# One transformer layer on one core: transposes set one by one between filler products, the causal mask between two score products, another order of the first loads with zero products ahead, and another order of the second and third norm

## The chip, the core and the metric

The kernel runs on one core of one Trainium2 chip. The time is the device time of one execution in microseconds (us), and the one compared is the median of several executions. The engines are named as the profile names them: PE multiplies matrices (PEld loads its weights), DVE and ACT work element by element, POOL and SP issue transfers here, and each of the five follows its own list of instructions in order, waiting on semaphores of the others.

## What is computed

The input is 1024 tokens of 1024 channels. The reference, cut to what matters:

```python
h = rmsnorm(x, g_pre_mix)
proj = h @ w_in                                   # u_pool (512) and q, k, v (8 heads of 64)
y_pool = multiscale_pool(u_pool, ...) @ w_br_pool
# stick-breaking attention, strictly causal, per head:
z = (q @ k.T) / 8
log_1mb = where(mask, log_sigmoid(-z), 0)
tail = cumsum(log_1mb, reverse=True) - log_1mb
o = where(mask, exp(log_sigmoid(z) + tail), 0) @ v
y_sb = o @ w_br_sb
gates = sigmoid(h @ w_gate + b_gate)
x = x + rmsnorm((gates[:1024] * y_pool + gates[1024:] * y_sb) @ w_out, g_post_mix)
h2 = rmsnorm(x, g_pre_mlp)
x = x + rmsnorm(square(relu(h2 @ w_up)) @ w_down, g_post_mlp)
```

## The kernel before, in words

**Number format.** Every large matrix and every activation is split into a part `hi` (a cast, ACT) and a rest `lo` (a subtraction, DVE). One product of the model is then three products on PE, `hi` by `hi`, `lo` by `hi` and `hi` by `lo`, all added into one PSUM bank (`mm3`, lines 105 to 114). A dense product of one weight tile with 512 tokens takes eight such steps (`dense_steps`), 24 matmuls. Channels lie on the partitions, tokens on the free axis, in two halves of 512 tokens (`h` is 0 or 1).

**Stages.** Everything is one straight program, but the order in which the instructions stand on each engine is made by a scheduler that simulates the program when it is built; the order of the code is a priority to it, and `issue_after(i)` forbids it to put an instruction ahead of `i`.

1. *First projection* (`phase_in`, from line 250). SP loads `vt` (gains), then in turn pieces of the first weight tile `u0` and tiles of `x` (eight of 128 by 512 for each half), then the tiles `u1` and `u2` whole. POOL loads the constants `eye`, `eyeb`, `maskb`, `rcnt` and `wm`. For each of the eight `k`, ACT makes `hT_hi` (L280), DVE `hT_lo` (L281), ACT a square (L287), which DVE adds up. PE runs the products of `u0`, `u1`, `u2` (tiles `du`, `zu`) with the first half, then with the second, and in between the sum of squares (`ms`) and the transpose of the row factors (`rt`).
2. *Pooling mixer* beside the last projections of this stage and the first `q`, `k`.
3. *Attention* (`phase_attention`). Heads 0 to 7, for each four pairs of query blocks, the longest first. `att_scores` makes the scores of one block: for each piece of at most 512 keys a product with `q`, one with `qs` (the halves of `q` exchanged), and for the last piece a third one that adds the mask (`eyeb` by `maskb`, L510). ACT makes two sigmoids (`T`, `F`), DVE a scan over `F` (L517) and a product (L518). `F` is one buffer, the score banks `z` are two. `att_out` then, per pair of key blocks `m`, transposes four (on the diagonal three) 128 by 128 squares of the two `T` tiles into the bank `at` (L534), lets `pump` run some filler work, splits `at` into `ahi` (ACT, L541) and `alo` (DVE, L542), and multiplies by `v` (four matmuls into `o`, L547).
   The *filler* is the dense products of the gates and of later heads' `q`, `k`, `v`. A credit of steps is given out: `w_out` steps (2.3) at each `m`, and the rest of the head's steps over the score blocks (`w_in`). Each filler step may not run ahead of the fourth last mark, a mark being set by the scores, the transposes and `o`.
4. *Branches and output projection* (`phase_post`): eight tiles `out` with each half. After a half is done, its `chain` runs beside the following products: norm 2 (`ms`, L762), residual, sum of squares, norm 3 (`ms`, L780), and the split into the operands of the MLP (`b_hi`, `b_lo`, lines 746 to 748). `beside` and `tick` tie the parts of the chain to steps of PE: the numbers behind `yield` are steps.
5. *MLP* (`phase_mlp`, `down`): the products of a seven-product scheme. The first 32 half products read `b11` (channels 0 to 511) and `b21` (512 to 1023) of the first half of the tokens, for each of 16 `up` tiles both; then come the sums and products of the other operands, then `w_down`, then the last norm.

Of the kernel before, what the change touches and what calls it, by code (L numbers as in the profile page):

```python
# [28 lines left out]
LAG = 4  # L29
P = 128  # L30
# [19 lines left out]
class Block:  # L50
    def __init__(self, tc, x, w, wmix, vec, eye, eyeb, maskb, rcnt, out):
# [9 lines left out]
        self.marks = []  # L61


    def prep(self, key, g, pieces=(), load=None, stash=None):
# [9 lines left out]
        for a, b in zip(edges, edges[1:]):  # L74
# [5 lines left out]
            for i in range(a, b, n):  # L80
                c = slice(i, i + n)
                nc.scalar.copy(hi[:, c], raw[:, c])  # L82
                nc.vector.tensor_sub(lo[:, c], raw[:, c], hi[:, c].bitcast(F32))  # L83
# [19 lines left out]

    def mm3(self, ps, terms, first=True, last=True):
        nc = self.nc
        n = len(terms)
        for i, (wh, wl, rh, rl) in enumerate(terms):
            if self.pin and len(self.marks) >= LAG:
                with self.tc.issue_after(self.marks[-LAG].ins):
                    nc.tensor.matmul(ps, wh, rh, start=first and i == 0, stop=False)  # L110
            else:
                nc.tensor.matmul(ps, wh, rh, start=first and i == 0, stop=False)  # L112
            nc.tensor.matmul(ps, wh, rl, start=False, stop=False)  # L113
            nc.tensor.matmul(ps, wl, rh, start=False, stop=last and i == n - 1)  # L114
# [54 lines left out]
    def build(self):  # L169
# [46 lines left out]

        nc.scalar.preload_act_table_set(TABLES)
# [6 lines left out]
        self.vt = cp.tile([P, N_VEC], F32, name="vt")  # L224
        nc.sync.dma_start(self.vt, self.vec)
        self.gn = cp.tile([P, 32], F32, name="gn")
        nc.vector.tensor_scalar(out=self.gn, in0=self.vt[:, 0:32], scalar1=-0.5, scalar2=None, op0=ALU.mult)
# [22 lines left out]
    def phase_in(self):  # L250
# [7 lines left out]
        todo = [(0, 0, 1), (0, 1, 1), (0, 2, 2)]  # L258
        self.prep(*self.order[0], pieces=(256, 512), load=lambda: load(*todo.pop(0)))
        self.next_prep = 1  # L260
        self.weights(("u", 1), 0)
        load(0, 4, 2)
        load(0, 6, 2)
        self.weights(("u", 2), 0)
        for k in range(0, NK, 2):
            load(1, k, 2)
        for t, src in zip((self.eye, self.eyeb, self.maskb, self.rcnt), self.consts):
            nc.gpsimd.dma_start(t, src)
# [75 lines left out]
        nc.gpsimd.dma_start(wm, self.wmix)  # L344
# [144 lines left out]
    def att_scores(self, h, i):  # L489
# [13 lines left out]
        for c, n in pieces:  # L503
# [4 lines left out]
            nc.tensor.matmul(z[:, c : c + n], qs[:, tt], k[:, c : c + n], start=False, stop=not last)  # L508
            if last:
                nc.tensor.matmul(z[:, w - P : w], self.eyeb, self.maskb, start=False, stop=True)  # L510
# [10 lines left out]
    def att_out(self, h, g, a):  # L521
# [4 lines left out]
        for m in range(g + 1):  # L526
# [4 lines left out]
            for b, (s, tt) in enumerate(((2 * m + 1, 0), (2 * m + 1, 1), (2 * m, 0), (2 * m, 1))):  # L531
                if diag and b == 0:
                    continue
# [723 lines left out]
```

## Time and profile before

| | us |
|---|---|
| median of three runs (lowest, highest) | 1316.82 (1315.09, 1317.61) |
| the profiled execution, its own time | 1318.3 |
| its span, first to last instruction | 1316.5 |
| PE busy | 1283.5 |
| DVE busy | 913.7 |
| ACT busy | 603.1 |

The profiled execution took 1.8 us more than its span, and 1.5 us more than the median. In the rows of a timeline the first number is the start in us from the span's beginning, the second the time until the last one of the row ended, then engine, line, operation, output and inputs, shape and count; the bracket tells how long the engine had stood idle, and who ended that. A matmul's time holds its way through the array; the pace of PE is read from one start to the next. In a table by windows the columns are the stretch, its length, the busy time of PE, PEld, DVE, ACT and POOL with their counts, the granted share of the PE clock, and the share and rate of the DMA engines. In the list of waits stand the waiting instruction, the one waited for, the total, the number of times and the longest.

### The profile page before, as it was taken

Reading aid. Unit: us, or ns where it says so; the run is one execution under the profiler, and the core shown is the slowest. Engines: PE = TensorE matmul, PEld = TensorE weight load, DVE = VectorE, ACT = ScalarE, POOL = GpSimd, SP = SyncE. Lnnn points to the kernel's source line nnn. Section 1 sums busy time; section 2 is a strip of 40 time slices with the busy share of each in tenths; the row PEclk is TensorE's granted clock in tenths of the full one; section 3 lists DMA queues with packets and bytes.
Section 4 is the critical chain, followed back from the end, with each engine's and each line's share of the span. In section 5 each row is a group of like instructions: output and inputs, shape, how many; then the busy total and the mean of one; then the engine's idle time right before and its main releaser. Section 6 shows DMA issues by size and latency. Waiting matters only on the chain.

```text
span 1316.5 us, 16672 instructions
## 1 busy us (share of the span) xinstructions
PE 1283.5 (97%) x6200; PEld 1069.4 (81%) x6200; DVE 913.7 (69%) x1234; ACT 603.1 (46%) x921; POOL 141.2 (11%) x281
## 2 busy tenths in 40 slices
PE   7999999998999999999999999999999999999995
PEld 5888888887888888888878887888888888888885
DVE  7686586676676664663577959877775654776975
ACT  7144455454555543223345736554465433344341
POOL 0001202100211222100001002211121000001000
PEclk9999999999999999999999999999999999999998
DMA  6243635623746969543146667766559555557741
GB/s 220 65 160 109 209 98 160 129 64 72 153 130 196 258 212 243 176 161 111 51 173 224 193 238 247 249 204 204 192 192 356 188 185 200 195 178 243 238 159 64
DMA packets 75089, 233.79 MB, mean 178 GB/s; under 512 B 8448, under 2 KB 10768, under 8 KB 72832
## 3 DMA queue, kind: packets, MB, share of 16 engines
q1 hardware_dynamic: 47216, 143.70, 33.2%
q0 software_dynamic: 27216, 88.50, 22.3%
q8 instruction: 49, 0.80, 0.2%
q10 hardware_dynamic: 576, 0.52, 0.1%
q14 instruction: 32, 0.26, 0.1%
HBM read 178.16 MB, written 83.89 MB: 199 GB/s over the span
## 4 chain that ended last, share of the span: by engine, by line
PE 82%; DVE 9%; issue 3%; ACT 2%; DMA 2%; SPq 0%; POOL 0%; DVEq 0%; ACTq 0%; POOLq 0%
PE d L112 18%; PE d L113 18%; PE d L114 18%; PE dg L110 4%; PE dg L114 4%; PE dg L113 4%; PE o L547 3%; PE at L534 2%; DVE F L517 2%; PE dqk L114 1%; PE dqk L113 1%; DVE T L518 1%; PE dqk L110 1%; PE z L505 1%; PE z L508 1%
## 5 line engine op out<-in xcount | busy, mean ns | idle before, releaser
L113 PE MATMUL d<-blo,whi 128*128 128x512 f32 (+1 forms) x456 | 172.7, 379 | 0.0
L114 PE MATMUL d<-bhi,wlo 128*128 128x512 f32 (+1 forms) x456 | 171.9, 378 | 0.0
L112 PE MATMUL d<-bhi,whi 128*128 128x512 f32 (+1 forms) x456 | 168.6, 378 | 0.0
L517 DVE TENSOR_TENSOR_SCAN F<-F,one 128x896 f32<-128x896 f32 (+3 forms) x64 | 86.8, 1357 | 46.5 <-ACT F L515 46.0
L82 ACT CAST whi<-wraw 128x512 fp32r<-128x512 f32 (+2 forms) x93 | 71.1, 791 | 82.1 <-PE d L113 30.8
L110 PE MATMUL dg<-hT_hi,whi 128*128 128x512 f32 x256 | 106.0, 414 | 0.0
L114 PE MATMUL dg<-hT_hi,wlo 128*128 128x512 f32 x256 | 101.2, 395 | 0.0
L113 PE MATMUL dg<-hT_lo,whi 128*128 128x512 f32 x256 | 100.6, 393 | 0.0
L83 DVE TENSOR_TENSOR wlo<-wraw,whi 128x512 fp32r<-128x512 f32 (+2 forms) x93 | 81.4, 897 | 27.3 <-ACT whi L82 27.2
L114 PEld LDWEIGHTS d<-bhi,wlo 128*128 128x128 f32 x456 | 85.8, 188 | 16.2 <-issue 0.2
L113 PEld LDWEIGHTS d<-blo,whi 128*128 128x128 f32 x456 | 85.7, 188 | 16.1 <-issue 0.2
L112 PEld LDWEIGHTS d<-bhi,whi 128*128 128x128 f32 x456 | 85.5, 188 | 16.0
L542 DVE TENSOR_TENSOR alo<-at,ahi 128x512 fp32r<-128x512 f32 (+1 forms) x80 | 50.5, 632 | 47.2 <-ACT ahi L541 46.5
L112 PE MATMUL d<-b_hi,whi 128*128 128x512 f32 x196 | 76.5, 394 | 3.6 <-ACT b_hi L747 2.7
L113 PE MATMUL d<-b_lo,whi 128*128 128x512 f32 x196 | 77.3, 396 | 0.0
L114 PE MATMUL d<-b_hi,wlo 128*128 128x512 f32 x196 | 75.6, 394 | 0.0
L1024 DVE TENSOR_TENSOR wlo<-slots_hi,whi 128x1024 fp32r<-128x1024 f32 x29 | 35.5, 1224 | 53.3 <-ACT whi L1022 53.3
L1022 ACT CAST whi<-slots_hi 128x1024 fp32r<-128x1024 f32 x29 | 30.5, 1052 | 83.2 <-PE d L113 63.7
L541 ACT CAST ahi<-at 128x512 fp32r<-128x512 f32 (+1 forms) x80 | 43.6, 544 | 48.8 <-PE at L534 47.8
L1022 ACT CAST whi<-slots_lo 128x1024 fp32r<-128x1024 f32 x27 | 28.4, 1053 | 72.9 <-PE d L113 59.2
L1024 DVE TENSOR_TENSOR wlo<-slots_lo,whi 128x1024 fp32r<-128x1024 f32 x27 | 33.0, 1222 | 36.8 <-ACT whi L1022 36.8
L514 ACT ACTIVATE T<-z 128x896 f32<-128x896 f32 (+3 forms) x64 | 42.3, 661 | 32.2 <-PE at L534 20.3
(302 smaller groups left out, 3305.0 us busy)
## 6 DMA issues: line engine op xcount, KB each, us to landing
wraw<-w SPq DMA_DIRECT2D x82, 512.0 KB, 4.3
wscr<-w POOLq DMA_DIRECT2D x24, 1024.0 KB, 9.8
ext_b<-ascr SPq DMA_DIRECT2D x40, 512.0 KB, 4.5
gscr<-gs POOLq DMA_DIRECT2D x32, 256.0 KB, 4.7
gate<-gscr POOLq DMA_DIRECT2D x16, 512.0 KB, 3.6
pscr<-p SPq DMA_DIRECT2D x32, 256.0 KB, 3.6
braw<-w SPq DMA_DIRECT2D x16, 512.0 KB, 5.6
ascr<-c POOLq DMA_DIRECT2D x32, 256.0 KB, 4.8
```

Of the source, the lines that this page charges most:

```text
L82: nc.scalar.copy(hi[:, c], raw[:, c])
L83: nc.vector.tensor_sub(lo[:, c], raw[:, c], hi[:, c].bitcast(F32))
L110: nc.tensor.matmul(ps, wh, rh, start=first and i == 0, stop=False)
L112: nc.tensor.matmul(ps, wh, rh, start=first and i == 0, stop=False)
L113: nc.tensor.matmul(ps, wh, rl, start=False, stop=False)
L114: nc.tensor.matmul(ps, wl, rh, start=False, stop=last and i == n - 1)
L514: nc.scalar.activation(tl[:, :w], z[:, :w], AF.Sigmoid)
L517: nc.vector.tensor_tensor_scan(fr, fr, self.one1.to_broadcast([P, w]), 1.0, ALU.mult, ALU.mult)
L541: nc.scalar.copy(hi[:, c0:], at[:, c0:])
L542: nc.vector.tensor_sub(lo[:, c0:], at[:, c0:], hi[:, c0:].bitcast(F32))
L1022: last_split[0] = nc.scalar.copy(hi, src).ins
L1024: last_split[1] = nc.vector.tensor_sub(lo, src, hi.bitcast(F32)).ins
```

## The change

It has five parts.

1. *First loads.* `u0`, `u1` and `u2` are loaded in three pieces each, in turn with `x`, their first pieces by POOL; the first tile of `x` leads SP's queue, ahead of `vt`; the constants and `wm` go behind `x` on SP. The splits of the weights follow piece by piece.
2. *Zeros first.* DVE clears a tile, and PE multiplies it by itself nine times (128 by 512, bf16, into a bank that nobody reads) at the very beginning.
3. *Attention, transposes.* Only the first transpose of a group stands by itself; each of the others is put right behind one of the next filler matmuls (`between`), and the filler matmul after it may not pass it. What is left over after `pump` is issued then. `w_out` goes from 2.3 to 3.3.
4. *Attention, mask.* The mask product stands between the products with `q` and `qs` of the last piece, not behind both.
5. *Norms 2 and 3 and the start of the MLP.* For the first half, the scaling of channel block `e` in norm 3 may not run ahead of the split of block `e - 2` (`done[-2]`), so that splits and scalings alternate; the sum of norm 3 is put three steps earlier (`yield 28`); for the second half, the scaling and residual of norm 2 may not run ahead of the last weight split so far (`last_lo`). The first four half products of the MLP are both `b11` ones of the tiles 0 and 1, then both `b21` ones.

```diff
@@ mm3
         for i, (wh, wl, rh, rl) in enumerate(terms):
-            if self.pin and len(self.marks) >= LAG:
-                with self.tc.issue_after(self.marks[-LAG].ins):
-                    nc.tensor.matmul(ps, wh, rh, start=first and i == 0, stop=False)
...
+            after = self.marks[-LAG].ins if self.pin and len(self.marks) >= LAG else None
+            for j, (a, b) in enumerate(((wh, rh), (wh, rl), (wl, rh))):
+                with self.behind(after):
+                    m = nc.tensor.matmul(ps, a, b, start=first and i + j == 0, stop=last and i == n - 1 and j == 2)
+                after = None
+                if self.between:
+                    with self.behind(m.ins):
+                        after = self.between.pop(0)().ins
@@ phase_in
-        todo = [(0, 0, 1), (0, 1, 1), (0, 2, 2)]
-        self.prep(*self.order[0], pieces=(256, 512), load=lambda: load(*todo.pop(0)))
...
+        for g in range(3):
+            load_w(nc.gpsimd, g, 0, 256)
+        load(0, 0, 1)
+        nc.sync.dma_start(self.vt, self.vec)
...
+        load(0, 1, 1)
+        load_w(nc.sync, 0, 256, 512)
+        load(0, 2, 1)
+        load_w(nc.sync, 1, 256, 512)
+        load_w(nc.sync, 2, 256, 512)
+        load(0, 3, 1)
+        load_w(nc.sync, 0, 512, 1024)
         load(0, 4, 2)
+        load_w(nc.sync, 1, 512, 1024)
+        load_w(nc.sync, 2, 512, 1024)
         load(0, 6, 2)
...
         for t, src in zip((self.eye, self.eyeb, self.maskb, self.rcnt), self.consts):
-            nc.gpsimd.dma_start(t, src)
+            nc.sync.dma_start(t, src)
+        zero = pa.tile([P, H], BF16, name="zero")
+        nc.vector.memset(zero, 0.0)
+        idle = self.zps.tile([P, H], F32, name="idle", tag="o", bufs=1)
+        for _ in range(9):
+            nc.tensor.matmul(idle, zero[:, :P], zero, start=True, stop=True)
@@ att_scores
-            nc.tensor.matmul(z[:, c : c + n], qs[:, tt], k[:, c : c + n], start=False, stop=not last)
             if last:
-                nc.tensor.matmul(z[:, w - P : w], self.eyeb, self.maskb, start=False, stop=True)
+                nc.tensor.matmul(z[:, w - P : w], self.eyeb, self.maskb, start=False, stop=False)
+            nc.tensor.matmul(z[:, c : c + n], qs[:, tt], k[:, c : c + n], start=False, stop=True)
@@ att_out
-            for b, (s, tt) in enumerate(((2 * m + 1, 0), (2 * m + 1, 1), (2 * m, 0), (2 * m, 1))):
-                if diag and b == 0:
-                    continue
-                t = nc.tensor.transpose(at[:, b * P : b * P + P], a[tt][:, s * P : s * P + P], self.eye)
-            self.marks.append(t)
+            self.marks.append(turn(int(diag)))
+            self.between = [functools.partial(turn, b) for b in range(int(diag) + 1, 4)]
             self.pump(self.w_out)
+            while self.between:
+                self.between.pop(0)()
@@ phase_attention
-        self.w_out = 2.3
+        self.w_out = 3.3
@@ chain
+            with self.tc.issue_after(self.last_lo) if h else contextlib.nullcontext():
...
-        yield 31
+        yield 28
...
+                with self.tc.issue_after(done[-2]) if e > 1 else contextlib.nullcontext():
+                    m = norm(e)
+                done.append(self.fill_operand(("b11", "b21")[e // 4], e % 4, m))
@@ phase_mlp
-        for i in range(16):
+        for n, (i, j) in enumerate([(0, 0), (1, 0), (0, 1), (1, 1)] + [(i, j) for i in range(2, 16) for j in range(2)]):
```

The order of the built programs shows three places that matter here. The first is SP's queue at the very beginning (`x_...` and `wraw` are the tiles of `x` and the raw weights, the last number is the shape). Before:

```order
L225 DMA vt<-vec 128x52
L76 DMA wraw<-w 128x256
L256 DMA x_184<-x 128x512
L76 DMA wraw<-w 128x256
L256 DMA x_184<-x 128x512
L76 DMA wraw<-w 128x512
L256 DMA x_184<-x 128x1024
L76 DMA wraw<-w 128x1024
L256 DMA x_184<-x 128x1024 x2
```

The same place on SP in the changed kernel:

```order
L261 DMA x_182<-x 128x512
L281 DMA vt<-vec 128x52
L261 DMA x_182<-x 128x512
L276 DMA wraw<-w 128x256
L261 DMA x_182<-x 128x512
L276 DMA wraw<-w 128x256 x2
L261 DMA x_182<-x 128x512
L276 DMA wraw<-w 128x512
L261 DMA x_182<-x 128x1024
L276 DMA wraw<-w 128x512 x2
L261 DMA x_182<-x 128x1024
```

The third tile of `x` now comes alone and before any piece of 512 columns, and three further weight pieces stand on POOL's queue, where the constants stood.

The second place is PE in the fifth head, which has, with the first, the least filler (32 steps): the scores of 384 and of 512 keys (`z`), the products with `v` (`o`), transposes (`at`) and filler (`dg`). Before:

```order
L534 MATMUL at<-eye,T 128x128 x3
L505 MATMUL z<-k_2569,q_2441 128x384
L508 MATMUL z<-k_2569,qs_2562 128x384
L510 LDWEIGHTS eyeb
L510 MATMUL z<-maskb,eyeb 128x128
L505 MATMUL z<-k_2569,q_2441 128x512
L508 MATMUL z<-k_2569,qs_2562 128x512
L510 LDWEIGHTS eyeb
L510 MATMUL z<-maskb,eyeb 128x128
L547 MATMUL o<-ahi,v_1_2913 128x256
L547 MATMUL o<-ahi,v_0_2953 128x256
L547 MATMUL o<-alo,v_1_2913 128x256
```

In the changed kernel, from behind the scores of 384 keys of the same head and the four products `o` that follow them, to the scores of 512:

```order
L573 MATMUL at<-eye,T 128x128 x2
L117 MATMUL dg<-hT_lo_249,whi 128x512
L573 MATMUL at<-eye,T 128x128
L117 MATMUL dg<-hT_hi_248,wlo 128x512
L573 MATMUL at<-eye,T 128x128
L117 MATMUL dg<-hT_hi_248,whi 128x512
L117 MATMUL dg<-hT_lo_249,whi 128x512
L117 MATMUL dg<-hT_hi_248,wlo 128x512
L117 MATMUL dg<-hT_hi_289,whi 128x512
L544 MATMUL z<-k_2606,q_2466 128x512
L548 LDWEIGHTS eyeb
L548 MATMUL z<-maskb,eyeb 128x128
```

The two blocks of scores, which followed each other directly, now have four products `o`, a group of transposes and seven filler matmuls between them. Over the whole attention, 240 runs of transposes stand where 83 stood: 192 of one and 48 of two, where there were 46 of four, 33 of three, one of two and three of one.

The third place is PE where the MLP begins (with buffer numbers: each `d_...` is the bank of one half product, `whi_6015` and `whi_6040` are the tile `up` 0, `whi_6060` and `whi_6085` the tile 1). Before:

```order
L112 MATMUL d_6071<-b0_hi_5885,whi_6015 128x512
L112 MATMUL d_6096<-b0_hi_5885,whi_6015 128x512
L112 MATMUL d_6122<-b0_hi_5885,whi_6060 128x512
L112 MATMUL d_6148<-b0_hi_5885,whi_6060 128x512
L112 MATMUL d_6175<-b0_hi_5885,whi_6066 128x512
L112 MATMUL d_6196<-b0_hi_5885,whi_6066 128x512
L113 MATMUL d_6071<-b0_lo_5886,whi_6015 128x512
```

And in the changed kernel:

```order
L117 MATMUL d_6096<-b0_hi_5897,whi_6040 128x512
L117 MATMUL d_6127<-b0_hi_5897,whi_6085 128x512
L117 MATMUL d_6096<-b0_lo_5898,whi_6040 128x512
L117 MATMUL d_6096<-b0_hi_5897,wlo_6041 128x512
L117 MATMUL d_6096<-b0_hi_5897,whi_6040 128x512
L117 MATMUL d_6127<-b0_lo_5898,whi_6085 128x512
L117 MATMUL d_6127<-b0_hi_5897,wlo_6086 128x512
```

Before, the second matmul in the row is that of `b21` with tile 0 and so needs channel block 4 of the operand; now the first two banks are both of `b11`, and block 4 is first needed 24 matmuls and one sum of squares later.

66 lines of the change are left out of this document (40 added, 26 removed).

## The prediction

> **What bounds the kernel now.** The page comes first: PE is busy nearly all the time, and the chain that ended last runs over PE.
>
> ```profile
> span 1316.5 us, 16672 instructions
> PE 1283.5 (97%) x6200; PEld 1069.4 (81%) x6200; DVE 913.7 (69%) x1234; ACT 603.1 (46%) x921; POOL 141.2 (11%) x281
> ```
>
> So the change can only gain where PE stands still, works at half pace, or pays more than a small matmul must. The list of PE's waits tells where it stands.
>
> ```profile
> PE du L112 <- ACT hT_hi L280: 8.1, 3, 5.8
> PE o L547 <- DVE alo L542: 3.9, 6, 1.3
> PE d L112 <- ACT b_hi L747: 2.7, 1, 2.7
> PE z L505 <- ACT F L515: 1.8, 2, 1.6
> PE at L534 <- DVE T L518: 1.0, 1, 1.0
> PE d L112 <- DVE u L931: 0.9, 1, 0.9
> ```
>
> The change touches the first five: the loads (`du`), the start of the MLP (`b_hi`), and the attention (`o`, `z`, `at`). Three places are read in the timeline. First PE's start.
>
> ```profile
> 5.82 0.79 PE L112 MATMUL du<-hT_hi,whi 128*128 128x512 f32 x1 [5.82 <-ACT hT_hi L280]
> 8.39 0.80 PE L112 MATMUL du<-hT_hi,whi 128*128 128x512 f32 x1 [0.56 <-ACT hT_hi L280]
> 12.13 0.80 PE L112 MATMUL du<-hT_hi,whi 128*128 128x512 f32 x1 [1.73 <-ACT hT_hi L280]
> 15.64 0.63 PE L113 MATMUL zu<-hT_lo,whi 128*128 128x512 f32 x1
> 16.07 0.51 PE L112 MATMUL du<-hT_hi,whi 128*128 128x512 f32 x1
> 16.41 0.40 PE L114 MATMUL zu<-hT_hi,wlo 128*128 128x512 f32 x1
> 16.64 0.39 PE L112 MATMUL zu<-hT_hi,whi 128*128 128x512 f32 x1
> ```
>
> From start to start a matmul of 512 columns takes 0.43 us until about 16.3 (15.64 to 16.07) and 0.23 from then on (16.41 to 16.64): PE begins at half pace. Six matmuls are done before 12.13 and nine more start before 16.41. At full pace these 15 are worth 3.4 us, so 13.0 us are lost at the start; behind it PE no longer waits. What it waits for comes from ACT; the first row below is of DVE and shows when the first small transfer was there.
>
> ```profile
> 2.51 0.18 DVE L227 TENSOR_SCALAR gn<-vt 128x32 f32<-128x32 f32 x1 [1.50 <-DMA vt<-vec]
> ...
> 5.05 0.72 ACT L280 ACTIVATE hT_hi<-x,gn 128x512 fp32r<-128x512 f32 x1 [1.37 <-DMA x<-x]
> 7.61 0.72 ACT L280 ACTIVATE hT_hi<-x,gn 128x512 fp32r<-128x512 f32 x1 [1.03 <-DMA x<-x]
> 9.91 0.62 ACT L82 CAST whi<-wraw 128x512 fp32r<-128x512 f32 x1 [1.06 <-DMA wraw<-w]
> 11.35 1.34 ACT L280 ACTIVATE hT_hi<-x,gn 128x512 fp32r<-128x512 f32 x2 [0.82 <-DMA x<-x]
> ```
>
> ACT in turn waits for transfers each time; the third tile of `x` is there at 11.35 only. Second, the fifth head, with the windows around it.
>
> ```profile
> 320.42 0.23 PE L510 MATMUL z<-maskb,eyeb 128*128 128x128 bf16 x1
> 322.22 0.50 PE L505 MATMUL z<-k,q 128*128 128x512 f32 x1 [1.57 <-ACT F L515]
> 322.83 0.48 PE L547 MATMUL o<-ahi,v 128*128 128x256 f32 x2
> 324.60 0.79 PE L547 MATMUL o<-alo,v 128*128 128x256 f32 x2 [1.28 <-DVE alo L542]
> ...
> 320.00:323.40 3.40, 1.75 (x11) 0.96 (x8) 2.43 (x3) 1.29 (x2) 0.00 (x0) 1.00 0.84 107
> 323.50:330.30 6.80, 5.71 (x21) 5.12 (x21) 2.60 (x4) 0.59 (x1) 0.41 (x2) 0.50 0.54 98
> 330.30:333.70 3.40, 3.40 (x20) 2.89 (x19) 2.49 (x4) 2.75 (x6) 0.22 (x1) 1.00 0.02 5
> ```
>
> Two waits of 1.57 and 1.28 us lie close together, and behind them the granted clock is 0.50 for 6.8 us, which costs another 3.4: this one place costs 6.3 us. Third, the start of the MLP, where 2.69 us of waiting are followed by 3.4 us at clock 0.50.
>
> ```profile
> 681.09 0.39 PE L112 MATMUL d<-b_hi,whi 128*128 128x512 f32 x1
> 684.17 1.57 PE L112 MATMUL d<-b_hi,whi 128*128 128x512 f32 x5 [2.69 <-ACT b_hi L747]
> ...
> 681.07 1.05 ACT L82 CAST whi<-wraw 128x1024 fp32r<-128x1024 f32 x1 [0.44 <-PE d L113]
> ...
> 685.30:688.70 3.40, 3.40 (x10) 2.65 (x9) 3.40 (x6) 0.38 (x1) 0.00 (x0) 0.50 0.12 33
> ```
>
> **The change part by part.** *First loads and zeros.* Ahead of the third tile of `x`, and with it, some 1.9 MB were asked for before (by shape: 1.5 on SP, 0.4 of constants on POOL), and it was there at 11.35, 8.8 us behind the first transfer of all (2.51). Now it is 1.28 MB; at the same rate that is 6.0 us, so 8.5, and with one `hT_hi` (0.72) and a short cast PE gets its third channel block at about 9.4. Until then the order gives it eight matmuls (two blocks of `u0`, two matmuls of `u1`), 1.8 us at full pace, so 7.6 are lost. Behind that, ACT and DVE have a piece of each weight and a tile of `x` ready faster than PE takes nine matmuls (2.0 us), so I see no further wait. That is 5.4 less than 13.0. The nine zero products at half pace (0.43 each, 3.9 us) lie in time in which PE waits anyway (to 5.82); they cost nothing unless the first tile lands before 5, and then at most 0.5. They decide whether PE is at full pace at 9.4. In the window from 320.0 PE was busy for 1.75 of 3.40 us and lost its clock, so a few waits between 5 and 9 could undo the zeros' work: the next 11 matmuls would then take 2.5 us more. I take **-5.0**; the ends are -2.5 (half pace remains, or transfers in small pieces are slower) and -6.5. The Trainium skill, "TensorE: Matmul & The Clock Gate" (section "What's actually happening"), says that the clock is gated by a free-running window of 3413 ns, full after a busy window and half after an idle one; the stretch of 6.8 us at 0.50 is two such windows, so the trace agrees, and by that rule 3.9 us of zeros fill most of one window wherever it begins.
>
> *Transposes.* What one costs between fillers can be read, since a few stand so already.
>
> ```profile
> 120.71 0.39 PE L114 MATMUL dg<-hT_hi,wlo 128*128 128x512 f32 x1
> 120.94 0.27 PE L534 MATMUL at<-eye,T 128*128 128x128 f32 x1
> 120.97 0.47 PE L110 MATMUL dg<-hT_hi,whi 128*128 128x512 f32 x1
> 121.28 0.39 PE L113 MATMUL dg<-hT_lo,whi 128*128 128x512 f32 x1
> ...
> 237.74 0.60 PE L534 MATMUL at<-eye,T 128*128 128x128 f32 x4
> 238.09 0.48 PE L110 MATMUL dg<-hT_hi,whi 128*128 128x512 f32 x1
> 238.41 0.40 PE L113 MATMUL dg<-hT_lo,whi 128*128 128x512 f32 x1
> ...
> L534 PE MATMUL at<-eye,T 128*128 128x128 f32 x288 | 45.9, 276 | 1.0 <-DVE T L518 1.0
> ```
>
> The lone one: from 120.94 to 121.28 pass 0.34, less 0.227 for the filler, 0.12 us (0.119 unrounded). The four in a row: 0.67 less 0.227, 0.11 each. The filler behind a transpose starts late by the same amount whether one or four went before: what is paid is the load of the next weights, which has only the short transpose to hide behind. So spacing saves nothing; 192 lone ones at 0.008 more are **+1.7** (ends 0 and +2.5, by the difference of the two rows). The mask is a small matmul too: before, the load of what followed it was exposed, now that of `qs`; I cost it at 0 (at worst 64 times 0.01, +0.6).
>
> *Waits in the attention.* The last transpose now has seven fillers behind it until `o` where it mostly had six: 0.23 us more cover for `ahi` and `alo`. In the fifth head, counting the order at 0.227, 0.12 and 0.11 a matmul, the scores of 768 keys stood 2.8 us ahead of those of 512, which wait for their bank; now 7.1 us. I expect the waits there, 2.85 us, to shrink to 1 or 1.5, too little to lose the clock: -5.0. But `w_out` of 3.3 takes ten steps of filler per head from the scores, and in the fifth head leaves none, so other places must get tighter; the smaller waits of before (about 4 us in the list besides) may grow. I set +1.0. With the transposes the attention gives **-2.3**, with ends of -8 (all waits and the half clock gone) and +6 (one more such place of 6.3 us).
>
> *Norms and MLP.* Before, the second matmul could have started at 681.32 and started at 684.17: 2.85 us, and 3.4 us at half clock cost 1.7, in all 4.55. Now it needs the weight tile 1, whose cast ran from 681.07 to 682.1: 0.8 us of wait remain, and DVE's alternating splits, one scaling and one split per block against 1.4 us of PE for six matmuls, keep up to within some 0.3. **-3.5**; ends -2 (clock still lost) and -4.3. What comes late next is DVE with its splits of the second half and the first sums of the MLP, behind which PE already waits 0.9 for `u`; of the gain up to 1 us can go there, which is in the range. `last_lo` puts weight splits ahead of norm 2 on DVE: the scalings queue behind them, and only the chain of the second half waits, which starts earlier now.
>
> The sum is -5.0 - 2.3 - 3.5 = -10.8 on the profiled 1318.3, 1307.5; that execution is 1.5 above the median, so I forecast 1316.8 - 10.8 = **1306.0**.
>
> **The rivals.** *The loads hide (faster).* If the weights of a transpose and of the filler behind it both loaded beside a stream of 512 columns, a transpose would cost little more than the 0.03 us between its start and the filler's (120.94 to 120.97) instead of 0.11: 288 of them save up to 23 us, 240 first ones of a run about 19, so 1306 - 1.7 - 19 = 1285. The lone one at 120.94 and the four at 237.74 speak against it. The Trainium skill states the mechanism on the same page ("Step-by-step: what each phase is for"): PE pulls weight loads ahead of matmuls in flight, into a background buffer. The trace agrees for the fillers and shows for the transposes that the load behind the small one is not hidden. Chance 0.05.
>
> *The start's gain is swallowed.* The chain of waits runs over DVE and POOL's transfers in the pooling stage:
>
> ```profile
> 76.96 6.17 DMA yscr<-win
> ```
>
> If this stretch does not move with PE, PE comes to the first heads 5 us early and waits there (it waits 1.0 for `T` already): 1306 + 5 = 1311. Against it: what is stored there comes out of PE's pooling products, so it should move as well. Chance 0.17.
>
> *The scores starve (slower).* With ten steps less between them, the scores of several heads come in pairs; `F` is one buffer, so the second pair waits for the scan, twice in one window, and the clock halves as at 323.5. Each such place costs 6.3. If the fifth head's remains (no -5.0) and two more come, the attention gives +12.6 + 1.7, and with the other two parts 1316.8 + 14.3 - 8.5 = 1322.6. It decides from about two places more than now. For it: the first and the fifth head have 32 steps of filler only, and the first credit leaves 2 steps or none for scores. Against it: in the other heads 44 to 52 steps remain. Chance 0.08.
>
> *The attention gets worse by as much as the ends gain*, without halved clocks: 1313 to 1319, chance 0.10.
>
> **How the numbers follow.** Forecast 0.60 (1300 to 1310), starved 0.08, swallowed 0.17, level 0.10, hidden loads 0.05. A measurement of this kernel can tell about 0.2%, 2.6 us, from no change. Faster: 0.60 + 0.17 + 0.05 + 0.02 of the level case = 0.84; within 0.2%: 0.06; slower: 0.08 + 0.02 = 0.10. The range leaves out the hidden loads, the starved case and the upper half of the level case (0.18): the three lower ends together, 1316.8 - 6.5 - 8 - 4.3, are 1298, and since they will hardly all meet, it goes from 1299 to 1316.
>
> **What would show it.** Right: `du` waits once or twice and PE is at pace 0.23 by about 9; lone transposes take 0.12; no window at 0.50 between 300 and 700; the wait for `b_hi` is under 1 us. Wrong: total PE time of `at` falls by 15 us or more; several windows at 0.50 in the attention; new waits for `T` or `alo` between 90 and 125; `d` waiting for DVE by 2 us or more around 770 to 790.

## The result: 1331.2 us, slower by 1.1%, and the profile after

The changed kernel took 1331.19 us (median of four runs, 1329.89 to 1332.69) against 1316.30 for the kernel before, a ratio of 1.0108 with a 95% interval of 1.0092 to 1.0123. The forecast was 1306.0 with a range of 1299 to 1316: the sign was wrong. The profiled execution took 1329.9 us; its page says:

```profile
span 1328.1 us, 16702 instructions
...
PE 1289.0 (97%) x6209; PEld 1065.1 (80%) x6209; DVE 912.7 (69%) x1239; ACT 602.1 (45%) x925; POOL 139.8 (11%) x279
```

PE is as full as before, so the loss does not show here. It shows in the list of PE's waits (waiting instruction, the one waited for, total, times, longest):

```profile
PE o L591 <- DVE alo L586: 14.4, 15, 2.9
PE d L117 <- ACT oh L699: 3.0, 1, 3.0
PE at L573 <- DVE T L557: 2.3, 2, 2.1
...
PE dqk L117 <- DVE wlo L85: 1.1, 1, 1.1
...
PE du L117 <- ACT hT_hi L319: 0.4, 1, 0.4
```

The 8.1 us for `hT_hi` have become 0.4, and the 2.7 for `b_hi` are gone. But `alo` has risen from 3.9 us in 6 waits to 14.4 in 15, and a wait that was not there at all, for `oh`, has come in. To see where the time went, the same instruction is looked up in the timelines of both kernels. In the kernel before, the first score, the first branch product with `oh`, and the first MLP product with `t_hi`:

```profile
86.26 0.40 PE L505 MATMUL z<-k,q 128*128 128x512 f32 x1
...
516.08 0.39 PE L112 MATMUL d<-oh,whi 128*128 128x512 f32 x1
...
774.58 0.39 PE L112 MATMUL d<-t_hi,whi 128*128 128x512 f32 x1
```

The same in the changed kernel, with the first MLP product (`b_hi`, 681.09 before) between them:

```profile
80.82 0.40 PE L544 MATMUL z<-k,q 128*128 128x512 f32 x1
...
529.88 0.97 PE L117 MATMUL d<-oh,whi 128*128 128x512 f32 x3 [2.98 <-ACT oh L699]
...
697.23 0.62 PE L117 MATMUL d<-b_hi,whi 128*128 128x512 f32 x2
...
787.71 0.39 PE L117 MATMUL d<-t_hi,whi 128*128 128x512 f32 x1
```

The changed kernel is 5.4 us ahead at the first score and 13.8 behind at the first `oh`: 19.2 us are lost between. Another 2.3 go until `b_hi` (16.1 behind), then 3.0 come back until `t_hi` and 1.5 from there to the end (11.6 behind by the spans). In these two traces the start gained 5.4 us and the MLP 4.5, a little more than was forecast; the attention and the passage behind it lost 21.5, more than twice as much.

Most of the 19.2 us is waiting: PE's waits of over 0.15 us rise from 7.6 to 22.3 us (+14.7). The transposes, with what they delay in the matmul behind them, take 34.6 us, 2.2 more than the same transposes in their old order (32.4, taken from the trace of e1 below, which has no half clock there). What is left is, by difference, half clock and slower matmuls right behind a wait. The clock of the changed kernel is 0.50 in four windows, from 107.9, 179.6, 323.0 and 531.2 (two of them below, as rows of the table by windows); before, there were 6.8 us from 323.5 and 3.4 from 685.3.

```profile
179.62:183.03 3.41, 3.41 (x10) 2.64 (x10) 0.74 (x2) 0.59 (x1) 0.00 (x0) 0.50 0.95 294
...
531.19:534.60 3.41, 3.41 (x8) 2.73 (x9) 3.30 (x3) 1.48 (x2) 0.00 (x0) 0.50 1.07 330
```

How a wait for `alo` arises is best read at one group of transposes, the first one for the longest blocks of the seventh head. In the kernel before, ACT and DVE ran there (ACT's row first):

```profile
417.20 0.59 ACT L541 CAST ahi<-at 128x512 fp32r<-128x512 f32 x1 [0.65 <-PE at L534]
...
417.28 0.95 DVE L518 TENSOR_TENSOR T<-T,F 128x767 f32<-128x767 f32 x1
418.26 0.42 DVE L552 TENSOR_TENSOR oT<-o,ou 64x256 f32<-64x256 f32 x1
418.71 0.69 DVE L542 TENSOR_TENSOR alo<-at,ahi 128x512 fp32r<-128x512 f32 x1
```

`ahi` started as soon as the transposes were done, DVE had a product and a sum ahead of `alo`, and PE did not wait. The same group in the changed kernel, PE first, then ACT, then DVE:

```profile
419.80 0.27 PE L573 MATMUL at<-eye,T 128*128 128x128 f32 x1
...
420.14 0.27 PE L573 MATMUL at<-eye,T 128*128 128x128 f32 x1
...
420.49 0.27 PE L573 MATMUL at<-eye,T 128*128 128x128 f32 x1
...
420.83 0.27 PE L573 MATMUL at<-eye,T 128*128 128x128 f32 x1
...
423.64 0.40 PE L591 MATMUL o<-ahi,v 128*128 128x256 f32 x2
426.35 0.51 PE L591 MATMUL o<-alo,v 128*128 128x256 f32 x2 [2.31 <-DVE alo L586]
...
421.00 1.13 ACT L84 CAST whi<-wraw 128x512 fp32r<-128x512 f32 x2
422.03 0.59 ACT L585 CAST ahi<-at 128x512 fp32r<-128x512 f32 x1
...
421.14 1.76 DVE L556 TENSOR_TENSOR_SCAN F<-F,one 128x768 f32<-128x768 f32 x1 [0.49 <-ACT F L554]
422.93 0.96 DVE L557 TENSOR_TENSOR T<-T,F 128x767 f32<-128x767 f32 x1
423.81 0.69 DVE L507 TENSOR_TENSOR gs<-dg,rb 128x512 f32<-128x512 f32 x1
424.41 1.28 DVE L85 TENSOR_TENSOR wlo<-wraw,whi 128x512 fp32r<-128x512 f32 x2
425.61 0.69 DVE L586 TENSOR_TENSOR alo<-at,ahi 128x512 fp32r<-128x512 f32 x1
```

The four transposes now take 1.03 us from the first to the last, where a row of four takes 0.33. Two weight casts have got ahead of `ahi` on ACT, and when `ahi` ends at 422.6 a scan is under way on DVE, with a product, a gate's product and two weight rests queued before `alo`. PE has 3.2 us of work from the last transpose to the first product with `alo`; it would need 5.5.

Over all 80 groups (three or four transposes each) the timelines give, in the mean, before and after: from the first transpose to the last 0.53 and 1.00 us; PE's work from the last one to the first product with `alo`, the wait itself left out, 3.94 and 3.58; from the first transpose to the end of `alo` 3.16 and 3.57. Each of these means moved by half a microsecond or less, but the waits come from a few groups: 15 of the 80 wait for `alo`, the longest for 2.9 us.

### The profile page after: what moved, and what is told of

The parts are those of the page before. It is cut to its first block, busy times and chain, and to the rows that moved or that the text cites. A ratio compares the mean times of both kernels' runs of the same rounds, so it can differ in the third digit from the quotient of the medians.

```text
span 1328.1 us, 16702 instructions
## 1 busy us (share of the span) xinstructions
PE 1289.0 (97%) x6209; PEld 1065.1 (80%) x6209; DVE 912.7 (69%) x1239; ACT 602.1 (45%) x925; POOL 139.8 (11%) x279
## 4 chain that ended last, share of the span: by engine, by line
PE 81%; DVE 10%; ACT 3%; issue 3%; DMA 2%; SPq 0%; DVEq 0%; ACTq 0%; POOL 0%; POOLq 0%
PE d L117 58%; PE dg L117 9%; PE dqk L117 3%; DVE F L556 3%; PE o L591 2%; PE dv L117 2%; PE at L573 2%; PE zu L117 2%; PE du L117 2%; DVE T L557 1%; DVE wlo L85 1%; DVE alo L586 1%; ACT F L554 1%; DMA wraw<-w 1%; DMA gscr<-gs 1%
## 5 line engine op out<-in xcount | busy, mean ns | idle before, releaser
L117 PE MATMUL dg<-hT_lo,whi 128*128 128x512 f32 x256 | 105.8, 413 | 0.0
L117 PE MATMUL dg<-hT_hi,wlo 128*128 128x512 f32 x256 | 105.4, 412 | 0.0
L84 ACT CAST whi<-wraw 128x512 fp32r<-128x512 f32 (+1 forms) x88 | 67.6, 801 | 70.2 <-PE d L117 36.9
L117 PEld LDWEIGHTS d<-bhi,whi 128*128 128x128 f32 x456 | 85.5, 188 | 16.1
L85 DVE TENSOR_TENSOR wlo<-wraw,whi 128x512 fp32r<-128x512 f32 (+1 forms) x88 | 77.2, 903 | 27.0 <-ACT whi L84 27.0
L585 ACT CAST ahi<-at 128x512 fp32r<-128x512 f32 (+1 forms) x80 | 43.6, 545 | 68.3 <-PE at L573 67.9
L573 PE MATMUL at<-eye,T 128*128 128x128 f32 x288 | 70.0, 272 | 2.3 <-DVE T L557 2.3
```

The costliest lines, as they stand in the source:

```text
L85: self.last_lo = nc.vector.tensor_sub(lo[:, c], raw[:, c], hi[:, c].bitcast(F32)).ins
L117: m = nc.tensor.matmul(ps, a, b, start=first and i + j == 0, stop=last and i == n - 1 and j == 2)
L573: return nc.tensor.transpose(at[:, b * P : b * P + P], a[tt][:, s * P : s * P + P], self.eye)
L585: nc.scalar.copy(hi[:, c0:], at[:, c0:])
```

## The experiments

Four questions were open: which part of the attention's change costs the time, what makes `alo` late, why `oh` is waited for, and whether the gains at the two ends are real without the rest. Twelve kernels answer them. Ratios are against the kernel before, with 95% intervals; differences in us are worked out from ratios with 1316.3 us (the changed kernel: +14.2).

**e1: the attention as before, both ends changed.**

`att_out`, `mm3` and `att_scores` are those of the kernel before; with them:

```diff
-        self.w_out = 3.3
+        self.w_out = 2.3
```

> The changed kernel with its attention put back as it was before: transposes in a row, mask behind both score products, w_out 2.3; first loads, zeros, norms and the start of the MLP stay changed. The traces of before and after put the start at -5.4 us and the norms with the MLP at -4.1. Theory A (the ends gain on their own, the attention loses on its own): 1316.3 - 9.5 = 1306.8, within 1.5. Rival (part of the loss, the wait of 3.0 us for oh and the half clock behind it, comes from the earlier start, because transfers keep their time): 1311 to 1312, with a wait of PE for oh in the list. Rival (the scheduler makes another order of the attention for any change of the start): anything from 1302 to 1315, with waits in the attention that differ from those of before.

1309.77 us, ratio 0.9957 (0.9943 to 0.9970), -5.7 us. The waits for `alo` are those of before, and there is none for `oh`:

```profile
PE o L586 <- DVE alo L581: 3.9, 6, 1.3
PE at L573 <- DVE T L556: 2.1, 1, 2.1
```

So the loss belongs to the attention's part, all of it: the two kernels lie 19.9 us apart. The time is 3 us above theory A, more than the 1.5 that it allowed, so the ends gain less than the traces of before and after made believe (e12 shows a part of the reason). The profiled execution, which kept the full clock from 4.3 us to its last 11, was the lowest with 1307.4. Another piece is seen: in the first head PE now waits 2.1 us for `T` instead of 1.0, so 1.1 us of the start's gain are given back there.

**e2: `w_out` back at 2.3, the transposes still strung.**

```diff
-        self.w_out = 3.3
+        self.w_out = 2.3
```

> The changed kernel with w_out back at 2.3, all else as changed. Theory W (w_out of 3.3 takes the filler from between the scores, so that scans and products bunch on DVE and alo stands behind them): the waits for alo fall from 14.4 us to about 4 and the time to 1308 to 1310. Rival S (the strung transposes themselves make alo late, since the last one comes some 0.7 us later with less filler behind it): with w_out 2.3 there is still less filler behind the last transpose, so waits for alo stay at 14 us or grow, and the time is 1331 or up to 1340.

1323.46 us, ratio 1.0060 (1.0045 to 1.0074), +7.9. Neither theory alone: 6.3 us of the loss are gone, and against e1, which differs by the strung transposes and by the mask, 13.6 remain. Its waits:

```profile
PE o L591 <- DVE alo L586: 5.3, 15, 0.9
PE d L117 <- ACT oh L699: 3.5, 1, 3.5
PE o L591 <- ACT ahi L585: 2.8, 5, 0.8
```

Many short waits for `alo` and `ahi`, and the one for `oh`. In its trace 8.3 us are lost against e1 by the last `o`, another 5.4 by the first product with `oh`.

**e3: transposes in a row, `w_out` 3.3.** The old `att_out` and `mm3` with the new `w_out` and mask.

```diff
-            self.marks.append(turn(int(diag)))
-            self.between = [functools.partial(turn, b) for b in range(int(diag) + 1, 4)]
+            for b, (s, tt) in enumerate(((2 * m + 1, 0), (2 * m + 1, 1), (2 * m, 0), (2 * m, 1))):
...
+            self.marks.append(t)
```

> The changed kernel with the transposes in a row again, mask between the score products and w_out 3.3 as changed. Theory W (w_out): waits for alo stay near 14 us, the time 1326 to 1331. Rival S (spacing): waits for alo fall to 4 us or less, since ahi can start three fillers earlier, and the time is 1306 to 1312.

1320.49 us, ratio 1.0042 (1.0028 to 1.0056), +5.5: 8.7 us of the loss are gone. Against e1 `w_out` (with the mask) costs 11.2 us.

```profile
PE o L586 <- DVE alo L581: 7.7, 12, 1.3
PE z L543 <- ACT F L553: 3.1, 5, 1.0
```

The work behind the last transpose has grown, as meant (4.13 us in the mean, 3.92 in e1), and still the waits grew: the cast `ahi` starts over 0.3 us behind the last transpose in 48 of the 80 groups, 35 in e1. Three clock windows at half pace come with it, from 107.4, 312.2 and 325.8; the trace of e1 has none in the attention. So W and S both hold in part: the two changes cost 13.6 and 11.2 us alone and 19.9 together, so 4.9 us of what each costs is the same loss.

**e4: the mask behind both score products.**

```diff
-                nc.tensor.matmul(z[:, w - P : w], self.eyeb, self.maskb, start=False, stop=False)
-            nc.tensor.matmul(z[:, c : c + n], qs[:, tt], k[:, c : c + n], start=False, stop=True)
+            nc.tensor.matmul(z[:, c : c + n], qs[:, tt], k[:, c : c + n], start=False, stop=not last)
...
```

> The changed kernel with the mask product behind both score products again, all else as changed. Theories W and S: the mask costs 0.12 us a piece in both traces wherever it stands, so 1331 within 2. Rival M (the mask between makes the scores end later or changes the scheduler's order of DVE): 1322 or less.

1331.06 us, ratio 1.0120 (1.0103 to 1.0137): no different from the changed kernel. The mask costs nothing, as forecast.

**e5: transposes in a row, one filler step ahead of them.**

```diff
+            self.pump(1.0)
             for b, (s, tt) in enumerate(((2 * m + 1, 0), (2 * m + 1, 1), (2 * m, 0), (2 * m, 1))):
...
-            self.pump(self.w_out)
+            self.pump(self.w_out - 1.0)
```

> The kernel of e1 (ends changed, attention as before) with one thing more: one of the 2.3 filler steps of each group is issued ahead of the transposes, which stay in a row, so that 1.3 steps stand behind the last transpose as in e2. No transpose stands alone. Theory S1 (strung transposes lose because the last one comes three fillers later, and so less filler covers ahi and alo): the waits for ahi and alo and the wait for oh come as in e2, 1318 to 1324. Rival S2 (the loss is from the transposes standing alone or from the order that their pins force, not from the cover): as e1, 1308 to 1312.

1312.33 us, ratio 0.9972 (0.9962 to 0.9983), 2.0 us above e1. This looks like S2, but it does not decide: in the trace the work from the last transpose to the first `alo` product is 3.92 us in the mean, just as in e1. The scheduler arranged the step so that the mean cover stayed. Only the quarter of the groups with the least cover has lost some (1.5 us or less, 2.4 in e1), and the waits for `ahi` and `alo` rise from 3.9 us in 6 to 6.2 us in 17. e10 cuts the cover in another way.

**e6: the last three weight sums behind the last gate's store.**

```diff
-            next(self.wsums)
+            self.n_gate += 1
+            for _ in range({30: 0, 31: 0, 32: 3}.get(self.n_gate, 1)):
+                next(self.wsums)
```

> The changed kernel, with the last three transfers of weight sums (1 MB each) on POOL's queue put behind the last gate's store, not one behind each of the last three stores. Theory Q (the cast of oh waits for the last gate's store, which lies 11 us behind the 2 MB of sums ahead of it): the wait of 3.0 us for oh and the half clock behind it go, 1326 to 1328. Rival (the store is late because the last gate is late on PE, whatever is ahead of it): wait for oh stays within 1 us, time 1331.

1332.55 us, ratio 1.0123 (1.0109 to 1.0138): no gain. The wait for `oh` went, but at the same place PE now waits longer, for the first gate loads, which stand behind the 3 MB:

```profile
542.20 0.79 PE L117 MATMUL d<-oh,whi 128*128 128x512 f32 x1 [5.85 <-DVE t L726]
```

The place where the sums stand decides, but moving them by so little only moves the wait. How it looked in the changed kernel: on POOL the store of the last gate goes out at 517.82, and the cast of `oh`, which takes over the memory of the gate tiles, can start only when it has landed:

```profile
517.82 0.57 POOL L509 DMA_DIRECT2D gscr<-gs  x1 [4.08 <-ACT gs L508]
...
528.79 3.88 ACT L699 CAST oh<-oT 128x1024 fp32r<-128x1024 f32 x4 [9.96 <-DMA gscr<-gs]
```

Before, the same cast started at 513.04 after 4.96 us of such waiting, 3 us ahead of its first reader on PE.

**e9: the last three sums behind loads of later gates.** What e6 left open, with the sums where nobody waits.

```diff
-            next(self.wsums)
+            self.n_gate += 1
+            if self.n_gate < 30:
+                next(self.wsums)
@@ phase_post
             merge(e, p, q)
+            if 3 < e < 7:
+                with tc.issue_after(self.gate_load.ins):
+                    next(self.wsums)
```

> The changed kernel, with the last three transfers of weight sums (1 MB each) put behind loads of gates of the branches instead of between the last gate stores; in e6 they stood ahead of all the gate loads, and the wait for oh became one for the gates. Theory Q (PE waits at the start of the branches because POOL's queue carries 2 to 3 MB that nobody needs yet, just then): no wait for oh or t over 1 us in the list, half clock around 531 gone, 1326 to 1328. Rival (the last gates themselves come too late): a wait of 2 us or more remains there, 1330 or more.

1324.09 us, ratio 1.0057 (1.0039 to 1.0074), 6.7 us under the changed kernel. The store lands in 4.9 us instead of 11, the cast starts 6.4 us earlier, and `oh` is not in the list of waits any more; `alo` stays at 14.4.

```profile
517.50 0.54 POOL L510 DMA_DIRECT2D gscr<-gs  x1 [5.31 <-ACT gs L509]
...
522.40 3.91 ACT L702 CAST oh<-oT 128x1024 fp32r<-128x1024 f32 x4 [3.89 <-DMA gscr<-gs]
```

So theory Q holds. In the trace 5.8 us are won by the start of the output projection: the wait of 3.0, and the half clock and slower first products behind it.

**e7: the weight rests on POOL.**

```diff
-                self.last_lo = nc.vector.tensor_sub(lo[:, c], raw[:, c], hi[:, c].bitcast(F32)).ins
+                eng = nc.gpsimd if self.pin else nc.vector
+                self.last_lo = eng.tensor_sub(lo[:, c], raw[:, c], hi[:, c].bitcast(F32)).ins
```

> The changed kernel, with the rests of the weight splits (wlo, 0.69 us each) computed by POOL instead of DVE during the attention. Theory D (in the changed kernel alo comes too late because it stands on DVE behind scans, products, gate products and wlo, 2.9 to 3.0 us in the worst groups, of which wlo is 1.4): waits for alo fall from 14.4 us to 8 to 10, the time to 1322 to 1327. Rival (alo is late because ahi and the last transpose are late): waits for alo stay within 2 us of 14.4 and the time is 1329 or more. Third (POOL is too slow for it): new waits for wlo, 1331 to 1345.

1334.28 us, ratio 1.0135 (1.0118 to 1.0152): slower still, and no verdict on theory D, since something else came in. POOL takes 1.68 us for one, and meanwhile DVE's product `T` is held up; the waits for `alo` stay at 14.6 us. The groups of the attention by shape, in the changed kernel:

```profile
L586 DVE TENSOR_TENSOR alo<-at,ahi 128x512 fp32r<-128x512 f32 x48 | 33.1, 690 | 45.5 <-ACT ahi L585 43.6 <-POOL ahi L583 1.4
...
L557 DVE TENSOR_TENSOR T<-T,F 128x767 f32<-128x767 f32 x8 | 7.6, 954 | 0.1
```

and in e7:

```profile
L587 DVE TENSOR_TENSOR alo<-at,ahi 128x512 fp32r<-128x512 f32 x48 | 33.1, 689 | 51.9 <-ACT ahi L586 51.6
...
L558 DVE TENSOR_TENSOR T<-T,F 128x767 f32<-128x767 f32 x8 | 11.4, 1425 | 0.2
```

DVE's busy time between 86 and 516 us falls by 18.9 us only, not by the 34.0 that the rests took: its other work takes longer, `T` by 7.7 us and `k` by 2.7. And in the trace the time is not lost in the attention, which takes 433.9 us from the first score to the last `o` (435.1 in the changed kernel), but ahead of it: the first score comes 3.0 us later.

**e11: no weight rests in the attention.**

```diff
-                self.last_lo = nc.vector.tensor_sub(lo[:, c], raw[:, c], hi[:, c].bitcast(F32)).ins
-        self.prepped[key] = (hi, lo)
+                if not self.pin:
+                    self.last_lo = nc.vector.tensor_sub(lo[:, c], raw[:, c], hi[:, c].bitcast(F32)).ins
+        self.prepped[key] = (hi, hi if self.pin else lo)
```

> The changed kernel without the rests of the weight splits (wlo) that DVE computes in the attention, 48 of 0.68 us; the products read the hi part in their place, so this part of the computation is left out, and the time of PE stays the same. Theory D (in the changed kernel alo stands on DVE behind a queue of scan, product, gate product and wlo): waits for alo fall from 14.4 us to 8 to 11, time 1322 to 1327. Rival (the queue is set by ahi and by the scan, wlo only fills gaps): 13 us or more of waits for alo, 1329 or more.

1317.85 us, ratio 1.0014 (1.0004 to 1.0025), 12.4 us under the changed kernel. This kernel leaves out a part of the computation and only shows what PE waited for.

```profile
PE o L592 <- DVE alo L587: 9.0, 14, 1.7
PE d L118 <- ACT oh L700: 3.9, 1, 3.9
```

The waits for `alo` fall to 9.0, as theory D said; the time falls by more, because with the longest wait for `alo` now 1.7 us the clock was full from 4.2 us to 519.6. So the rests in DVE's queue ahead of `alo` are a part of what PE waited for. Nine us of waits remain without them.

**e10: `w_out` 1.3, transposes in a row.**

```diff
-        self.w_out = 2.3
+        self.w_out = 1.3
```

> The kernel of e1 with w_out of 1.3 instead of 2.3, transposes in a row. By the order of the built programs the work between the last transpose and the first product with alo is then 3.2 us in the mean, as in e2 with strung transposes (3.2), against 3.7 in e1. Theory S1 (strung transposes lose because less work covers ahi and alo): waits for ahi and alo of 8 us or more and 1316 to 1324. Rival S2 (they lose by something else, since filler taken from the cover goes between the scores and helps there): 1307 to 1312.

1321.59 us, ratio 1.0041 (1.0029 to 1.0053), 11.1 us above e1.

```profile
PE o L586 <- DVE alo L581: 7.1, 22, 1.0
...
PE dg L116 <- DVE v L496: 1.7, 1, 1.7
PE o L586 <- ACT ahi L580: 1.5, 5, 0.8
```

With the transposes in their old order, less filler behind the last one gives the many short waits for `alo` and `ahi` of e2 (8.6 us here, 8.1 there). The products with `v`, with the waits ahead of them, take 59.0 us instead of 49.3 in e1. That speaks for S1. It is no clean proof. The mean cover fell less than the order had promised: in the traces it is 3.92 us in e1, 3.69 here and 3.37 in e2. And the first head alone takes 5.0 us more than in e1, with waits for `v` and a half clock at 108.5. What stands is that 2.3 is the best of the three values tried: a step more (e3, with the new mask) and a step less for each group both cost 11 us.

**e8: one zero product instead of nine, on e1.**

```diff
-        for _ in range(9):
+        for _ in range(1):
```

> The kernel of e1 with one zero product at the start instead of nine. Theory Z (the zeros bring PE to full pace before the third block of channels; without them the first 3.4 us of real work run at half pace): full clock from about 9 to 13 us on, first scores 1.7 us later, 1311.5. Rival (the first products themselves bring the clock up as early): no change, 1309.8.

1309.20 us, ratio 0.9949 (0.9935 to 0.9963): no difference from e1 that can be told. The clock was full from 12.0 us instead of 4.3, but PE came to the first score only 1.1 us later (82.10 and 81.02): at half pace it fills time in which it would have waited for the next channels (behind 5.5 us it waits no more, where e1 waits three times, 1.6 us in all). The gain of the start is that of the order of the loads.

**e12: norms and start of the MLP alone, on the kernel before.** The diff is that of `chain` and `phase_mlp` in the section on the change.

> The kernel before with the new order of the norms 2 and 3 and of the start of the MLP alone. The prediction took -3.5 (ends -2 and -4.3), of which 1.7 is a half clock; the traces of e1, e5 and e8 show the way from the first product of the MLP to the second operand shorter by 1.9 to 3.3 us and what follows by another 0.9. So 1311.9 to 1313.7 if it stands alone; rival (these were gains that only an earlier attention brings, or luck of the half clock): 1315 or more.

1314.08 us, ratio 0.9987 (0.9977 to 0.9997), -1.7 us. A real gain, but under what was expected and under the smaller end of the prediction (-2). The wait for `b_hi` is gone, and 26 us later there is a new one, for the cast of a weight tile:

```profile
PE d L112 <- ACT whi L82: 1.7, 1, 1.7
```

It was not there before; it is 1.9 us in e8, 0.8 in the changed kernel and 0.5 in e1, so the traces of after and e1 flattered this part. The start's share of e1 is then about 4.0.

## Why the prediction was wrong

*First loads and zeros, -5.0.* The size is right: -5.4 in the trace to the first score, of which 1.1 are lost again to `T` in the first head, and about -4.0 by e1 less e12. The part of the zeros in it is not: they do bring PE to full pace, but that was worth 1.1 us at the first score and nothing that can be told in the time (e8), where the prediction took 2.5 to hang on it.

*Transposes, +1.7.* Right (192 times 0.008 is rather 1.5): +2.2 by the count above, and a lone one still takes 0.12 (420.14 to 420.49, less 0.227). *Mask, 0.* Right (e4).

*Norms and MLP, -3.5.* The mechanism is right (the wait for `b_hi` is gone, block 4 is in time), the size too large: -1.7 by e12 (-0.4 to -3.0), since a new wait for `whi` takes some of it back. The half clock behind the old wait was entered as a fixed 1.7 us; it comes in some executions only (last section).

*Waits in the attention, -4.0, is the step that failed.* It had two terms, -5.0 for the fifth head and +1.0 for other places. The first came by half at most. All waits of the fifth head fell from 4.9 to 4.0 us, and its half clock from 6.8 to 3.4, not to none: the scores' waits for `F` have shrunk from 1.8 to 0.3 us, as was expected, but those for `alo` are 3.2 us as before, and the longest has grown from 1.28 to 1.84:

```profile
321.11 0.48 PE L591 MATMUL o<-alo,v 128*128 128x256 f32 x2 [1.84 <-DVE alo L586]
```

From its first score to that of the sixth head it takes 43.6 us instead of 45.2. The second term is the failure: from the first score to the last `o` the changed kernel loses 14.1 us (5.4 ahead, 8.6 behind), and with +2.2 for the transposes and -1.6 for the fifth head that leaves some 13 us at other places, not 1.0. There the waits rise from 2.7 to 15.3 us, and two windows at half clock come in. The reasoning went wrong at this sentence: "The last transpose now has seven fillers behind it until `o` where it mostly had six: 0.23 us more cover". That counted a typical group of PE's order. In the trace the mean cover fell by 0.36 us; and cover is only one side. The other is when `ahi` and `alo` are done, which depends on what stands before them on ACT and DVE, and neither queue was counted. Both halves of the edit push there: strung transposes end 0.5 us later and use up filler that covered the casts (13.6 us, e2 against e1, of which 8.3 fall in the attention and the rest in the passage behind it), and `w_out` 3.3 takes ten steps a head from between the scores (11.2 us, e3 against e1). That sigmoids, scans and products then come in front of the casts is read from the group shown and from the later `ahi` of e3; for the weight rests it is shown by e11. That the first costs so much through the cover is supported by e10, not proved. The higher `w_out` was to pay for the first half; by e2 it made the kernel 6.3 us slower instead.

*What was not foreseen at all* is the passage to the branches: 6.7 us (e9). The prediction has no term for it. The last gates' stores had come together at the end of the attention with 2 MB of weight sums between them on POOL's queue, and `oh` waits for the last store because it takes over memory of the tile that is stored.

*The rivals.* "The scores starve" had the right sign, but neither its mechanism nor its price: the score blocks that follow each other without filler between are 13 before and 14 after, and the waits are for `alo`, not for `F` (1.8 us before, 0.3 after). "The start's gain is swallowed" is true for 1.1 of 5.4 us. "The loads hide" did not happen. "Worse by as much as the ends gain" was the right direction with well under half of the size. Two of the signs listed as speaking against the forecast came: windows at 0.50 in the attention, and a wait for `T` at 107.4.

The kernel to keep is that of e1 or e8, with the attention as it was: 1309.8 and 1309.2 us.

## What to carry to other kernels

When work is moved between a producer on PE and its consumer, the cover has to be counted for every group and not for a typical one, and against the queues of the engines that stand between, in their order: here the mean over 80 groups moved by less than half a microsecond, while single groups waited up to 2.9 us. Filler is a fixed sum: a step given to one place is missing at another, and where a tuned value is found, a change that consumes filler has to bring its own. At the border of two stages, look up whose memory the next stage's first tiles take over, and what stands in the queue ahead of the transfer that frees it.

## What the runs showed of the hardware

*The half clock is a matter of where the window falls.* Before, e1, e8 and e12 run the same attention with the same two waits in the fifth head (1.57 to 1.61 and 1.27 or 1.28 us). In two of the traces they are followed by 6.8 us at half clock, in two by none. The windows of e1, with their borders worked out from the clock's changes, split the waits as 1.61 and 1.27:

```profile
314.90:318.31 3.41, 1.80 (x11) 1.24 (x9) 2.44 (x3) 1.64 (x3) 0.56 (x1) 1.00 0.79 135
318.31:321.72 3.41, 2.14 (x14) 1.66 (x13) 2.78 (x3) 0.43 (x2) 0.00 (x0) 1.00 1.11 202
```

The kernel before had 1.75 us of waiting in one window, and lost the clock:

```profile
320.08:323.50 3.42, 1.67 (x10) 0.88 (x8) 2.45 (x3) 1.29 (x2) 0.00 (x0) 1.00 0.86 112
323.50:326.91 3.41, 2.31 (x9) 2.12 (x10) 1.90 (x3) 0.58 (x1) 0.00 (x0) 0.50 1.02 187
```

In all 14 traces of this case every stretch between two changes of the clock is a whole number of such windows (3.41, 6.83, 102.40, 307.20 us). Adding up PE's idle time in each window of 3.41 us at full clock, and leaving out the last 30 us of each trace, over 1.92 us was always followed by a window at 0.50 (17 of 17), under 1.5 never, and between 1.5 and 1.92 it went both ways. The Trainium skill, "TensorE: Matmul & The Clock Gate" (section "What's actually happening"), has the window free-running, which agrees; that section speaks of an idle window as the cause of half clock, and here one that is idle for about half of its time is enough. So a half clock seen in one profile is worth its price only times its chance: the mean granted clock of single executions of the kernel before goes from 0.992 to 0.997, and the times with it from 1317.8 to 1319.4 us down to 1312.7 to 1315.8.

*POOL's arithmetic slows DVE's, by where the inputs lie.* In e7 the product `T`, both inputs in SBUF, took 1425 ns instead of 954 in the mean: the five of eight that ran beside a subtraction of POOL took 1454 to 1858 ns, the other three 948 to 956. `alo`, with one input in PSUM, took 689 and 690. The Trainium skill, "SBUF — State Buffer" (section "Who interferes with whom"), states this: an instruction of DVE with two SBUF inputs contends with one of GpSimd that reads SBUF, one with a single SBUF input does not, outside the two-port modes. The traces agree for these two; not every product beside POOL is slowed (of six 895 wide, five took 1105 to 1115 ns; the two without POOL took 1078 and 1092).
